# One load queue in the order of need, and x normalised between the steps of the context's projection

## The chip, the cores and the metric

The kernel runs on one core of a Trainium2 chip. The metric is the device time of one execution in microseconds, as the median of three runs. Engines are named as in the profile: PE is TensorE (PEld its weight load), DVE is VectorE, ACT is ScalarE, POOL is GpSimd, SP is SyncE; SPq and ACTq are the queues on which SP and ACT issue DMAs.

## The reference

Two transformer blocks on x (512 tokens by 1024), all in float32. The change touches only the beginning of the first one:

```
mod   = silu(c) @ w_ada + b_ada            # w_ada: 1024 x 6144, six vectors of 1024: shift, scale, ...
h     = rmsnorm(x,   g) * (1 + scale) + shift        # 512 x 1024, with c
h_ctx = rmsnorm(ctx, g) * (1 + scale) + shift        # 256 x 1024, with c_ctx
p     = h @ w_in,  p_ctx = h_ctx @ w_in              # w_in: 1024 x 10304
# columns of p: q, k, v, z, then xBC (a convolution of 5 taps over tokens, then silu), dt, gates
# then neighbourhood attention, a state-space scan seeded by the context's states, 16 experts;
# then a second block of two layers
```

The context is needed first: its B and its x columns of xBC give the states with which the scan of x begins.

## The kernel before, in words

Matrix products keep float32 precision by splitting both operands into a high and a low part; one "step" of the projection is three matmuls (high by high, low by high, high by low; `mm3`, L331 to L333) of one k-tile. `Stream` holds an ordered list of units (a set of weight columns with its steps). Raw weights (`raw`, 2 buffers) come by DMA on SPq; ACT makes the high part (`wh`, L200), DVE or, every second time once `pool_share` is 2, POOL the low part (`wl`, L220), a pair of k-tiles at a time, five pairs at most. `st.count` counts steps; `st.defer(n, f)` runs `f` n steps later, and all that `f` issues then stands in the in-order queues of its engines behind what was issued before. `st.wait = 14` keeps a pair from being split until its raw load was issued 14 steps ago, and `st.stop` with `pump_some` splits pairs by hand.

The order of units at the beginning: `ub` (B columns for the context, 32 steps of 256 tokens), `udt` (dt columns: 8 steps for the context, 8 for x), `us[0]` to `us[3]` (x columns of xBC for the context, 32 steps each), then `qk_unit(0)`, the first that needs x in earnest. After each half of a 32-step unit comes `conv` (L760 on ACT twice, then L765 on DVE eight times), and after the second half a Silu on ACT (L784).

Before the first step: `ident`, `va`, `vb`, the two tiles of ctx and the four of x are loaded on ACTq; the first 2048 columns of `w_ada` come on SPq as 16 tiles of 512 KB (`ada_load`, L667 to L671), in four groups along k. All six tiles are squared and normalised together (L701 to L705), transposed on PE (L716) to `cT` and `xT`, and `ada_mm` (L695) makes shift and scale, which L932 to L940 turn into columns. `modulate` (L730) then takes a tile k at a time: DVE scales and shifts (L732), ACT writes the high part (L737), DVE or POOL the low part (L738). For the context `pump_some` splits three further pairs of weights in between; for x, `modulate(0, ...)` calls `st.fill(1.0)` after each k, so that some three steps of `ub` run between two k.

The other 4096 columns of `w_ada` come in 16 tiles of 1 MB (`ada_load2`, L899) on ACTq; `ada_mm2(i)` (L905) multiplies tile i in between the steps: the first at step 20 (`ADA0`), one every 10 steps (`ADA`), tile i+3 being asked for 8 steps (`AL`) after tile i was used.

## Time and profile before

| what | us |
|---|---|
| median of 3 runs | 3430.79 (3430.62 to 3438.5) |
| the profiled execution, its own time | 3432.32 |
| its span in the trace | 3430.5 |
| PE busy in the span | 3208.5 (94%) |
| DVE, ACT, POOL busy | 1624.5, 1168.1, 554.2 |

Times inside the trace are counted from the start of the span; the execution's own time is 1.8 us longer than the span. The change lies in the first 5% of it. A PE that is busy need not be at its full clock: the granted clock (PEclk) is 1.00 at 2.4 GHz and 0.50 at 1.2 GHz.

### The profile page before, as it was taken

Reading aid. Unit: us, or ns where it says so; the run is one execution under the profiler, and the core shown is the slowest. Engines: PE = TensorE matmul, PEld = TensorE weight load, DVE = VectorE, ACT = ScalarE, POOL = GpSimd, SP = SyncE. Lnnn points to the kernel's source line nnn. Section 1 sums busy time; section 2 is a strip of 40 time slices with the busy share of each in tenths; the row PEclk is TensorE's granted clock in tenths of the full one; section 3 lists DMA queues with packets and bytes.
Section 4 is the critical chain, followed back from the end, with each engine's and each line's share of the span. In section 5 each row is a group of like instructions: output and inputs, shape, how many; then the busy total and the mean of one; then the engine's idle time right before and its main releaser. Section 6 shows DMA issues by size and latency. Waiting matters only on the chain. (4 is left out here: it accounts for less than half of the span.)

```text
span 3430.5 us, 42023 instructions
## 1 busy us (share of the span) xinstructions
PE 3208.5 (94%) x16365; PEld 2207.9 (64%) x16365; DVE 1624.5 (47%) x3113; ACT 1168.1 (34%) x2064; POOL 554.2 (16%) x371
## 2 busy tenths in 40 slices
PE   7999999999899898888889888999999999999998
PEld 4778877777678543324324224777888877788887
DVE  5745557676554410111011015776544467765444
ACT  4455545555323100100000003555433355543332
POOL 2232213444110100000000000241111103401111
PEclk9999999999999899999999999999999999999999
DMA  8622122222444799999999996212323221123232
GB/s 293 237 65 79 59 79 79 83 80 77 146 147 184 310 410 418 420 421 421 421 421 421 421 421 227 68 47 71 93 92 105 92 88 56 41 84 99 92 92 80
DMA packets 223389, 646.64 MB, mean 188 GB/s; under 512 B 17973, under 2 KB 110253, under 8 KB 171349
## 3 DMA queue, kind: packets, MB, share of 16 engines
q1 hardware_dynamic: 211176, 607.26, 46.6%
q10 hardware_dynamic: 12013, 36.69, 3.0%
q8 instruction: 129, 2.11, 0.3%
q14 instruction: 71, 0.58, 0.0%
HBM read 628.67 MB, written 15.21 MB: 188 GB/s over the span
## 5 line engine op out<-in xcount | busy, mean ns | idle before, releaser
L1968 PE MATMUL hd<-xw,xe 128*64 128x512 f32 x2048 | 462.8, 595 | 63.1 <-DMA xw<-in_w_up_dram 42.1
L220 DVE TENSOR_TENSOR wl<-raw,wh 128x1024 fp32r<-128x1024 f32 (+1 forms) x306 | 377.9, 1249 | 124.3 <-ACT wh L200 122.8
L200 ACT ACTIVATE wh<-raw 128x1024 fp32r<-128x1024 f32 (+1 forms) x349 | 343.4, 1003 | 212.2 <-PE psg L333 133.1
L331 PE MATMUL psg<-HA,wh 128*128 128x512 f32 (+1 forms) x1024 | 392.6, 383 | 0.0
L332 PE MATMUL psg<-HB,wh 128*128 128x512 f32 (+1 forms) x1024 | 387.7, 379 | 3.9 <-DVE HB L467 3.9
L333 PE MATMUL psg<-HA,wl 128*128 128x512 f32 (+1 forms) x1024 | 388.0, 379 | 0.0
L1968 PEld LDWEIGHTS hd<-xw,xe 128*64 128x64 f32 x2048 | 151.6, 137 | 363.4 <-issue 241.2
L2009 PE MATMUL down<-xw,hidT 128*64 128x512 f32 x1024 | 237.8, 600 | 36.5 <-DMA xw<-in_w_down_dram 36.4
L331 PE MATMUL psg<-h_hi,wh 128*128 128x512 f32 x584 | 255.3, 437 | 1.1 <-DVE vsb L1334 0.9
L333 PE MATMUL psg<-h_hi,wl 128*128 128x512 f32 x584 | 236.9, 406 | 0.0
L332 PE MATMUL psg<-h_lo,wh 128*128 128x512 f32 x584 | 236.5, 405 | 0.0
L332 PEld LDWEIGHTS psg<-HB,wh 128*128 128x128 f32 x1024 | 195.0, 190 | 38.6 <-DVE HB L467 4.7
L333 PEld LDWEIGHTS psg<-HA,wl 128*128 128x128 f32 x1024 | 194.6, 190 | 35.9
L331 PEld LDWEIGHTS psg<-HA,wh 128*128 128x128 f32 x1024 | 195.7, 191 | 33.8
L2009 PEld LDWEIGHTS down<-xw,hidT 128*64 128x64 f32 x1024 | 75.0, 137 | 188.1 <-issue 120.6
L2627 POOL TENSOR_TENSOR va<-va,ga 128x512 f32<-128x512 f32 x44 | 90.9, 2066 | 546.1 <-DVE va L2609 546.0
L2024 ACT ACTIVATE yh<-down,gcol 128x512 fp32r<-128x512 f32 x16 | 11.0, 686 | 489.4 <-PE down L2009 489.4
L1980 DVE TENSOR_TENSOR hid<-hid,hd 128x512 f32<-128x512 f32 x32 | 22.0, 687 | 314.0 <-PE hd L1968 313.9
L2043 POOL TENSOR_TENSOR Y<-Y,R 128x512 f32<-128x512 f32 x4 | 5.0, 1275 | 966.4 <-ACT tmp L2041 966.4
L220 POOL TENSOR_TENSOR wl<-raw,wh 128x1024 fp32r<-128x1024 f32 (+1 forms) x43 | 101.7, 2368 | 291.2 <-ACT wh L200 291.2
L331 PE MATMUL psg<-wh,hidh 128*128 128x512 f32 x352 | 139.5, 396 | 0.0
L333 PE MATMUL psg<-wh,hidl 128*128 128x512 f32 x352 | 139.2, 396 | 0.0
(487 smaller groups left out, 5979.3 us busy)
## 6 DMA issues: line engine op xcount, KB each, us to landing
xw<-in_w_gate_dram SPq DMA_DIRECT2D x128, 1024.0 KB, 19.8
xw<-in_w_up_dram SPq DMA_DIRECT2D x128, 1024.0 KB, 19.8
xw<-in_w_down_dram SPq DMA_DIRECT2D x126, 1024.0 KB, 19.8
raw<-in_w_up_dram SPq DMA_DIRECT2D x176, 256.0 KB, 3.7
raw<-in_w_in_dram SPq DMA_DIRECT2D x34, 1024.0 KB, 5.2
raw<-in_w_in_dram SPq DMA_DIRECT2D x96, 256.0 KB, 3.1
raw<-in_w_down_dram SPq DMA_DIRECT2D x44, 512.0 KB, 4.3
raw<-in_w_in_dram SPq DMA_DIRECT2D x33, 512.0 KB, 4.7
```

The source lines that it names most:

```text
L200: nc.scalar.activation(wh[:, :kn, :nco], src, AF.Copy)
L220: eng.tensor_tensor(wl[:, :kn, :nco], src, wh[:, :kn, :nco].bitcast(F32), op=ALU.subtract)
L331: nc.tensor.matmul(ps, l, r, start=first, stop=False, skip_group_check=skip)
L332: nc.tensor.matmul(ps, l, rh, start=False, stop=False, skip_group_check=skip)
L333: nc.tensor.matmul(ps, lh, r, start=False, stop=last, skip_group_check=skip)
L1968: P.matmul(ps[c][64 * e:64 * e + 64], xe[p // 2][k // 2 % 2][:, 2 * (k // 4) + k % 2, c0:c0 + 64], self.tiles[p, w, k, e][:, 512 * c:512 * ...
L1980: V.tensor_tensor(acts[p, c], acts[p, c], ps[c], op=ALU.mult)
L2009: P.matmul(down[h][64 * e:64 * e + 64], b[:, 64 * e:64 * e + 64], w[:, 1024 * r + 512 * h:1024 * r + 512 * h + 512], start=j == 0 and r == ...
L2024: S.activation(hi, down[h], AF.Copy, scale=gates[p])
L2043: G.tensor_tensor(o, o, R3[:, :512], op=ALU.mult)
L2627: G.tensor_tensor(v, v, g[j], op=ALU.mult)
```

## The change

All first loads go on SPq, in this order: `ident`, `va`, `vb`, ctx, then `w_ada` as 1 MB tiles of 128 rows by 2048 columns (six buffers; tiles 6 and 7 are issued after the matmuls of tiles 0 and 1), the two raw tiles of `ub`, and only then x. Before the first step only the context is squared, normalised and transposed. `kb.warm` adds five matmuls of `ident` by itself behind the last `ada` matmul and 14 behind the four transposes of L932. The vectors of shift and scale are made before the first pair of weights is split, and the low parts of the context alternate between DVE and POOL.

x is worked on inside the projection: squares at steps 14 to 20, its `rsqrt` at 26, the four row scalings (`by_r`) at 28 to 34, and `x_turn(k)` at steps 42, 45, ... 63. `x_turn` transposes one k into a PSUM bank of tag `m` (there are two), DVE scales and shifts from PSUM, ACT makes the high part, DVE or POOL the low one. The dt columns for x become a unit of their own, `udtx`, after `us[0]`, which loads and splits these weight columns a second time. The first `ada_mm2` moves from step 20 to step 48, the spacing from 10 steps to 8, and the first three `ada_load2` from before the first step to steps 26, 32 and 38.

```diff
--- before.py
+++ after.py
@@ -572,8 +572,8 @@
 LAG = 4
 RT = (12, 15)
 WAIT = 14
-ADA = 10
-ADA0 = 20
+ADA = 8
+ADA0 = 48
 CS = (20, 22, 50, 54)
 FN = 4.6
 ORD = "tsn"
@@ -589,8 +589,8 @@
 NT = ('o', 's', 'm', 's')
 ROT = "gsmgsms"
 AQ = 20
-AL = 8
-SX = 56
+AL = 4
+SX = 28
 VT_ = 't'
 VD = 16
 NG = 3
@@ -617,7 +617,7 @@
 
     keep = es.enter_context(tc.tile_pool(name="keep", bufs=1))
     ident = keep.tile([128, 128], F32, name="ident")
-    S.dma_start(ident, A["ident"])
+    nc.sync.dma_start(ident, A["ident"])
     kb.ident = ident
     wx = ExitStack()
     wp = wx.enter_context(tc.tile_pool(name="wp", bufs=1, reuse_waits="tile"))
@@ -656,26 +656,23 @@
     p0 = zero.enter_context(tc.tile_pool(name="p0", bufs=1, side="right"))
     va = p0.tile([128, 128], F32, name="va")
     vb = p0.tile([120, 128], F32, name="vb")
-    S.dma_start(va, A["vec_a"])
-    S.dma_start(vb, A["vec_b"])
-    xT = p0.tile([128, 8, T], F32, name="xT")
+    nc.sync.dma_start(va, A["vec_a"])
+    nc.sync.dma_start(vb, A["vec_b"])
+    xx = p0.tile([128, 4, D], F32, name="xx")
     cT = p0.tile([128, 8, TC], F32, name="cT")
     raw = ExitStack()
     p00 = raw.enter_context(tc.tile_pool(name="p00", bufs=1, side="right"))
-    aw = {}
-
-    def ada_load(kh):
-        for j in range(4):
-            t = p00.tile([128, 2, 512], F32, tag="aw", bufs=8, name="aw")
-            nc.sync.dma_start(t, A["w_ada"][256 * kh:256 * kh + 256, 512 * j:512 * j + 512].rearrange("(k p) f -> p k f", p=128))
-            aw[kh, j] = t
-
-    ada_load(0)
-    ada_load(1)
-    xt = p00.tile([128, 6, D], F32, name="xt")
-    for t in (4, 5, 0, 1, 2, 3):
-        src = A["x"][128 * t:128 * t + 128] if t < 4 else A["ctx"][128 * (t - 4):128 * (t - 4) + 128]
-        S.dma_start(xt[:, t], src)
+    xt = p00.tile([128, 2, D], F32, name="xt")
+    for t in range(2):
+        nc.sync.dma_start(xt[:, t], A["ctx"][128 * t:128 * t + 128])
+    aw = []
+
+    def ada_load(k):
+        aw.append(p00.tile([128, 4, 512], F32, tag="aw", bufs=6, name="aw"))
+        nc.sync.dma_start(aw[k], A["w_ada"][128 * k:128 * k + 128, :2048].rearrange("p (j f) -> p j f", f=512))
+
+    for k in range(6):
+        ada_load(k)
     tri = p1.tile([128, 3, 128], F32, name="tri")
     sel = p1.tile([128, 24], F32, name="sel")
     dtv, acs, dte, Eac, cdec = (p1.tile([128, 6, 64], F32, name=n_) for n_ in "dtv acs dte Eac cdec".split())
@@ -689,41 +686,51 @@
     S.activation(sil[:, :, 0:2].rearrange("p k v -> p v k"), cols[:, 112:128].rearrange("p (v k) -> p v k", v=2), AF.Silu)
     ada_ps = PS.bank([128, 512], F32, "o", "ada")
 
-    def ada_mm(kh):
-        for k in range(2):
-            for j in range(4):
-                P.matmul(ada_ps[32 * j:32 * j + 32], sil[:, 2 * kh + k], aw[kh, j][:, k],
-                         start=kh == 0 and k == 0, stop=kh == 3 and k == 1, skip_group_check=True)
-
     ss = p0.tile([128, 6], F32, name="ss")
-    junk = xT[:, 0:2].rearrange("p a b -> p (a b)")
-    for t in (4, 5, 0, 1, 2, 3):
-        S.activation(junk, xt[:, t], AF.Square, accum_out=ss[:, t:t + 1])
-    V.tensor_scalar(ss, ss, 1.0 / D, EPS, op0=ALU.mult, op1=ALU.add)
-    rs = kb.rsqrt(ss, 6, p0)
-    for t in (4, 5, 0, 1, 2, 3):
-        V.tensor_scalar(xt[:, t], xt[:, t], rs[:, t:t + 1], None, op0=ALU.mult)
-    ada_mm(0)
-    ada_load(2)
-    ada_mm(1)
-    ada_load(3)
+    junk = cT[:, 0:4].rearrange("p a b -> p (a b)")
+    for t in range(2):
+        S.activation(junk, xt[:, t], AF.Square, accum_out=ss[:, 4 + t:5 + t])
     S.dma_start(tri, A["tri"])
     S.dma_start(sel, A["sel"])
-    for n in range(12):
+
+    def row_r(t0, n):
+
+        v = ss[:, t0:t0 + n]
+        V.tensor_scalar(v, v, 1.0 / D, EPS, op0=ALU.mult, op1=ALU.add)
+        return kb.rsqrt(v, n, p0)
+
+    def by_r(x, r):
+        V.tensor_scalar(x, x, r, None, op0=ALU.mult)
+
+    rc = row_r(4, 2)
+    for t in range(2):
+        by_r(xt[:, t], rc[:, t:t + 1])
+    for n in range(4):
         ps = PS.bank([128, 512], F32, "gsm"[n % 3], "xTp")
         for i in range(4):
-            k, t = (2 * n + i // 2, 4 + i % 2) if n < 4 else (n - 4, i)
-            P.transpose(ps[:, 128 * i:128 * i + 128], xt[:, t, 128 * k:128 * k + 128], ident)
-        if n < 4:
-            o, v = cT[:, 2 * n:2 * n + 2].rearrange("p a b -> p (a b)"), ps
+            P.transpose(ps[:, 128 * i:128 * i + 128], xt[:, i % 2, 256 * n + 128 * (i // 2):256 * n + 128 * (i // 2) + 128], ident)
+        o = cT[:, 2 * n:2 * n + 2].rearrange("p a b -> p (a b)")
+        if n % 2:
+            V.tensor_copy(o, ps)
         else:
-            o, v = in_time(xT[:, n - 4]), ps.rearrange("p (r g c) -> p r g c", g=8, r=8)
-        if n % 2:
-            V.tensor_copy(o, v)
-        else:
-            S.activation(o, v, AF.Copy)
-    ada_mm(2)
-    ada_mm(3)
+            S.activation(o, ps, AF.Copy)
+    for k in range(8):
+        for j in range(4):
+            P.matmul(ada_ps[32 * j:32 * j + 32], sil[:, k], aw[k][:, j], start=k == 0, stop=k == 7, skip_group_check=True)
+        if k < 2:
+            ada_load(6 + k)
+    kb.warm("m", 5)
+
+    def x_turn(k):
+
+        ps = PS.bank([128, 512], F32, "m", "xTp")
+        for t in range(4):
+            P.transpose(ps[:, 128 * t:128 * t + 128], xx[:, t, 128 * k:128 * k + 128], ident)
+        o = cT[:, 2 * (k % 4):2 * (k % 4) + 2].rearrange("p a b -> p (a b)")
+        V.tensor_scalar(in_time(o), ps.rearrange("p (r g c) -> p r g c", g=8, r=8), gsc[:, 0, k:k + 1], shc[:, 0, k:k + 1],
+                        op0=ALU.mult, op1=ALU.add)
+        S.activation(h_hi[:, k], o, AF.Copy)
+        (G if k % 2 else V).tensor_tensor(h_lo[:, k], o, h_hi[:, k].bitcast(F32), op=ALU.subtract)
     mod0 = p0.tile([128, 512], F32, name="mod0")
     V.tensor_copy(mod0, ada_ps)
     raw.close()
@@ -735,7 +742,7 @@
             if k < 7:
                 scale(k + 1)
             S.activation(hi[:, k], src[:, k], AF.Copy)
-            (G if k % 2 or v else V).tensor_tensor(lo[:, k], src[:, k], hi[:, k].bitcast(F32), op=ALU.subtract)
+            (G if k % 2 else V).tensor_tensor(lo[:, k], src[:, k], hi[:, k].bitcast(F32), op=ALU.subtract)
             each(k)
 
 
@@ -830,12 +837,12 @@
         ops += [lambda: stt(d, d, 1.0, s, op0=ALU.add, op1=ALU.mult),
                 lambda: stt(dtv[:, tk].rearrange("p t h -> p (t h)"), d, 2.0, xr, op0=ALU.mult, op1=ALU.add),
                 lambda: stt(th(na), dtv[:, tk], -1.0, alog[:, None, :].to_broadcast([128, nt, 64]), op0=ALU.mult, op1=ALU.mult),
-               ] + [None] * (16 if t0 else 38) + [
+               ] + [None] * (16 if t0 else 30) + [
                 sums, None, None,
                 lambda: S.activation(dte[:, tk], dte[:, tk], AF.Exp)]
         return ops
 
-    udt = Unit([([(0, A["w_in"][:, ODT:ODT + 128])], 8)], 128)
+    udt, udtx = (Unit([([(0, A["w_in"][:, ODT:ODT + 128])], 8)], 128) for _ in range(2))
 
     def spread(n0, ops, every=1):
         for i, f in enumerate(ops):
@@ -845,7 +852,7 @@
     def ev_dtc(ps):
         V.tensor_copy(dtT[:, T:], ps[:64, :TC])
         tt = lambda *a: V.tensor_tensor(*a, op=ALU.mult)
-        spread(14, dt_ops(4, 2) + [lambda: tt(ddc, dtv[:, 4:6], dte[:, 4:6]),
+        spread(6, dt_ops(4, 2) + [lambda: tt(ddc, dtv[:, 4:6], dte[:, 4:6]),
                                   lambda: tt(ddc[:, 0, :32], ddc[:, 0, :32], cdec[:, 5, :32]),
                                   lambda: tt(ddc[:, 1, 32:], ddc[:, 1, 32:], cdec[:, 4, 32:])])
     kb.group_b(udt, 0, act_c, TC, ev_dtc)
@@ -853,8 +860,9 @@
     def ev_dtx(ps):
         V.tensor_copy(dtT[:, :T], ps[:64, :T])
         spread(SX, dt_ops(0, 4))
-    kb.group_b(udt, 0, act_t, T, ev_dtx)
-    udt.steps = [(0, 2 * p + r, c, f) for p, r, c, f in udt.steps]
+    kb.group_b(udtx, 0, act_t, T, ev_dtx)
+    for u in (udt, udtx):
+        u.steps = [(0, 2 * p + r, c, f) for p, r, c, f in u.steps]
 
     def b_nat():
         def part(t):
@@ -924,12 +932,15 @@
 
     st.stop = True
     ub = xbc_unit(OB, 16, bcT, b_nat)
+    for t in range(4):
+        nc.sync.dma_start(xx[:, t], A["x"][128 * t:128 * t + 128])
     st.add(udt)
     us = [xc_unit(0)]
-    st.pump_some(1)
+    st.add(udtx)
     ptm = PS.bank([128, 512], F32, "t", "ptm")
     for m in range(4):
         P.transpose(ptm[:, 128 * m:128 * m + 128], mod0[:, 128 * m:128 * m + 128], ident)
+    kb.warm("m", 14)
     shc = p0.tile([128, 2, 8], F32, name="shc")
     gsc = p0.tile([128, 2, 8], F32, name="gsc")
     for v in (1, 0):
@@ -938,8 +949,7 @@
         V.tensor_tensor(shc[:, v].rearrange("p (j m) -> p j m", m=4), pv[:, 0:2], b4[:, 0], op=ALU.add)
         V.tensor_tensor(gsc[:, v].rearrange("p (j m) -> p j m", m=4), pv[:, 2:4], b4[:, 1], op=ALU.add)
         V.scalar_tensor_tensor(gsc[:, v], gsc[:, v], 1.0, cols[:, 0:8], op0=ALU.add, op1=ALU.mult)
-    for i in range(3):
-        ada_load2(i)
+    st.pump_some(1)
     modulate(1, cT, c_hi, c_lo, lambda k: k in (1, 3, 5) and st.pump_some(1))
     st.stop = False
     st.wait = WAIT
@@ -948,11 +958,20 @@
     kb.rot = ["g", "s"]
     st.defer(ADA0, lambda: ada_mm2(0))
     S.activation(alog, alog, AF.Exp)
-    modulate(0, xT, h_hi, h_lo, lambda k: st.fill(1.0))
-    zero.close()
+    for i in range(3):
+        st.defer(26 + 6 * i, lambda i=i: ada_load2(i))
+    rx_ = []
+    for t in range(4):
+        st.defer(14 + 2 * t, lambda t=t: S.activation(junk, xx[:, t], AF.Square, accum_out=ss[:, t:t + 1]))
+        st.defer(28 + 2 * t, lambda t=t: by_r(xx[:, t], rx_[0][:, t:t + 1]))
+    st.defer(26, lambda: rx_.append(row_r(0, 4)))
+    for k in range(8):
+        st.defer(42 + 3 * k, lambda k=k: x_turn(k))
     for g in range(1, 4):
         us.append(xc_unit(g))
         st.finish(us[g - 1])
+        if g == 1:
+            zero.close()
 
     shuf = [(i + 16) % 32 for i in range(32)]
     units, made, QK, VU, VT = {}, [0], {}, {}, {}
```

## Rows read from the trace of the kernel before

**Rows 1.** Busy time by stretch (us; count), TensorE clock, DMA share, GB/s.
```profile
18.00:36.00 18.00, 14.74 (x93) 7.21 (x93) 9.88 (x24) 5.70 (x10) 0.00 (x0) 0.91 1.05 385
41.00:47.00 6.00, 4.75 (x20) 4.46 (x21) 3.73 (x8) 3.65 (x7) 3.69 (x4) 0.50 1.01 426
47.00:54.00 7.00, 4.15 (x28) 3.35 (x27) 4.87 (x7) 3.54 (x7) 4.60 (x4) 0.99 0.49 141
54.00:57.40 3.40, 3.40 (x21) 3.18 (x23) 2.58 (x3) 1.67 (x4) 1.28 (x1) 0.51 0.52 201
60.00:100.00 40.00, 39.11 (x292) 30.55 (x292) 35.08 (x63) 18.52 (x25) 15.90 (x7) 1.00 0.79 284
100.00:140.00 40.00, 36.74 (x262) 27.58 (x261) 34.62 (x65) 19.32 (x28) 9.56 (x4) 0.96 0.80 280
```

**Rows 2.** DMA issues of the first 40 us: KB each, median us to landing.
```profile
aw<-in_w_ada_dram SPq DMA_DIRECT2D x16, 512.0 KB, 7.6
xt<-in_x_dram ACTq DMA_DIRECT2D x4, 512.0 KB, 8.1
```

**Rows 3.** Timeline, from the last w_ada tile to the context's last high part.
```profile
35.37 1.90 PE L695 MATMUL ada<-aw,sil 128*32 128x512 f32 x10 [1.56 <-DMA aw<-in_w_ada_dram]
38.12 1.06 ACT L200 ACTIVATE wh<-raw 128x1024 fp32r<-128x1024 f32 x1 [7.41 <-DMA raw<-in_w_in_dram]
39.21 1.22 DVE L220 TENSOR_TENSOR wl<-raw,wh 128x1024 fp32r<-128x1024 f32 x1 [1.21 <-ACT wh L200]
41.55 0.73 ACT L737 ACTIVATE c_hi<-cT 128x256 fp32r<-128x256 f32 x2 [2.37 <-DVE cT L732]
42.02 0.58 PE L331 MATMUL psc<-c_hi,wh 128*128 128x256 f32 x1 [3.31 <-ACT c_hi L737]
...
52.10 0.42 ACT L737 ACTIVATE c_hi<-cT 128x256 fp32r<-128x256 f32 x1 [1.72 <-DVE cT L732]
52.54 1.28 ACT L950 ACT_TABLE_LOAD   x1
```

**Rows 4.** Groups by line and shape, 0 to 160 us: busy us, mean ns.
```profile
L220 DVE TENSOR_TENSOR wl<-raw,wh 128x1024 fp32r<-128x1024 f32 x14 | 21.1, 1510 | 11.5 <-ACT wh L200 11.5
L765 DVE SCALAR_TENSOR_TENSOR xc<-psc,cw,xc 128x254 f32<-128x254 f32 x30 | 14.4, 482 | 1.1
L701 ACT ACTIVATE xT<-xt 128x1024 f32<-128x1024 f32 x6 | 6.3, 1054 | 0.6 <-DMA xt<-in_x_dram 0.4
L732 DVE TENSOR_SCALAR xT<-xT,gsc,shc 128x512 f32<-128x512 f32 x8 | 9.1, 1163 | 0.0
L705 DVE TENSOR_SCALAR xt<-xt,rs_y 128x1024 f32<-128x1024 f32 x6 | 4.1, 750 | 0.0
L722 DVE COPY xT<-xTp 128x512 f32<-128x512 f32 x4 | 2.7, 688 | 0.4 <-PE xTp L716 0.4
L563 DVE SCALAR_TENSOR_TENSOR rs_t<-rs_y 128x6 f32<-128x6 f32 x3 | 0.5, 166 | 0.1
L760 ACT ACTIVATE bcT<-psc,cols,cw 128x256 f32<-128x256 f32 x4 | 2.0, 548 | 0.0
```

**Rows 5.** Timeline of PE: transposes, two steps, step 80, the end of `us[3]`.
```profile
24.74 5.77 PE L716 MATMUL xTp<-ident,xt 128*128 128x128 f32 x48
...
63.82 0.28 PE L331 MATMUL psg<-c_hi,wh 128*128 128x256 f32 x1
64.17 0.28 PE L331 MATMUL psg<-c_hi,wh 128*128 128x256 f32 x1
...
90.45 1.06 PE L911 MATMUL ada<-aw,sil 128*32 128x512 f32 x8
...
154.32 0.28 PE L331 MATMUL psg<-c_hi,wh 128*128 128x256 f32 x1
```

**Rows 6.** Timeline of ACT: two issues of w_ada's later tiles.
```profile
103.15 0.33 ACTq L903 DMA_DIRECT2D aw<-in_w_ada_dram  x1
...
114.09 0.33 ACTq L903 DMA_DIRECT2D aw<-in_w_ada_dram  x1
```

## The prediction

> **What bounds the kernel now.** I read the stretches first. Until about 36 us the DMA engines are full (share 1.05, 385 GB/s) while PE, DVE and ACT have gaps: the beginning is bound by bytes [rows 1]. Then the timeline: PE gets the last `w_ada` tile at 35.37, starts the first step at 42.02, and ACT starts the context's last high part only at 52.10 [rows 3]. In 47 to 54 PE is busy 4.15 of 7 us: it follows the context's `modulate`, not its own speed; then it runs 3.4 us at half clock, and from 60 to 100 it is busy 39.1 of 40 us [rows 1]. The reader should see the column beside it: DVE is busy 35.1 of the same 40 us, and 34.6 of the next 40. There PE paces the kernel, but DVE follows with almost no slack. That decides this change, because it moves work onto DVE and hangs PE on it. All later stages only start earlier or later by what is won or lost here.
>
> **The loads.** Ahead of the last `w_ada` tile came 8 MB of `w_ada` and 3 MB of ctx and x; x (four tiles of 512 KB, 2.1 MB [rows 2]) now comes behind it. At 385 GB/s that is 5.4 us [rows 1]. The tiles are now 1 MB with 8 KB per partition; the stretch with such tiles in flight ran at 426 GB/s [rows 1], which on 8.4 MB would save 2.1 us more. Ends 5.4 and 7.5, taken 7.2, near the upper one: the tiles of that stretch have the shape of the new ones.
>
> **From the last tile to the end of the first half of `ub`.** Four matmuls remain after the last tile instead of ten, and the shift and scale are ready before the first pair of weights. But that pair still waits for its raw tile, which landed 2.75 us after the last `w_ada` tile, and then for wh 1.06, wl 1.22, one scaling, one high part (about 1 us): 6 us instead of 6.65 [rows 3]. Gain 0.7. In the half itself each two k cost wh, wl, a scaling and a high part in turn, 1.06 + 1.22 + 0.8 = 3.1 us, whoever makes the low part; 10.5 us pass between the first and the last high part [rows 3]. I give 0.5 for the low parts on DVE. The half ended near 54.0; it should end at 54.0 - 7.2 - 0.7 - 0.5 = 45.6, 8.4 us earlier. The 19 warm matmuls stand where PE waits for DVE and for the raw tile; if the five delay L932, by at most five transposes' worth, 0.6 us [rows 5].
>
> **x between the steps.** This is the step that costs. Between the end of the context's last high part (1.5 us before the half ends) and `x_turn(0)`, in order on ACT before the first convolution: a table load 1.28 (the Exp of `alog`), wh 1.06, a square 1.05, the convolution's first part 0.55: 3.9 us [rows 3, 4]. Then on DVE: eight taps of 0.48, 3.9; wl 1.2; `rsqrt` with its scaling, 12 small operations of 0.17, 2.0; wl 1.2; two row scalings of 0.75, 1.5; the second half's eight taps, issued at step 31, 3.9; two more row scalings, issued at 32 and 34, 1.5. Together 15.2 us [rows 3, 4]. So `x_turn(0)` can start at 45.6 - 1.5 + 3.9 + 15.2 = 63.2. PE needs for the 26 steps up to it 26 x 0.35 = 9.1 us [rows 5], and is there at 54.7. **It waits 8.5 us**, with all later steps queued behind four transposes.
>
> Then PE may do `x_turn(0)`, three steps and `x_turn(1)`, 2.05 us. Next come the transposes of dt at step 45, which need one of the two `m` banks, that is, the first scaling of x from PSUM. On DVE that stands behind wl of the second dt load, whose wh on ACT stands behind the Silu of B: table load 1.28, Silu 1.05, two wh 2.1, two issues 0.7, wl 1.2, the scaling 0.69, from 61.7 [rows 3, 4, 6]: 68.7. PE has been ready since 65.3: **3.4 us more.** By the clock rows a PE that has stood still 3.3 us resumes at 0.50 [rows 1, 3]; at that clock the 2.05 us are 4.1 and still fit. The Trainium skill, "TensorE: Matmul & The Clock Gate", section "HAM oscillation — how this bites in real kernels", says the same of idle gaps; by it the stall would be paid once more in slow matmuls, by these rows that payment lies inside the second wait.
>
> From step 45 to 80: 27 steps 9.5, six `x_turn` of four transposes 2.9, ten other transposes 1.2, four `ada_mm2` 4.2, eight steps of 512 tokens at 0.70, 5.6: 23.4 us [rows 5]. `x_turn(7)` needs the bank of `x_turn(5)`, whose scaling stands behind eight more taps (3.9) from step 55. Ends 0 and 5 (taps and what had queued), taken 3. Step 80 comes at 68.7 + 23.4 + 3 = 95.1, with four tiles of `ada_mm2` done; before it came at 90.45 with six [rows 5]. On equal footing (two of 1.06) that is 97.2: **6.8 us behind**, although the half ended 8.4 ahead. Of this, 3.9 us are the 32 transposes of x themselves (0.12 each [rows 5]), which lay under the loads before.
>
> The scaling of x is not dearer on DVE: a pass of 128x512 out of PSUM took 0.69, eight are 5.5, where the SBUF form here took 9.1 for eight [rows 4]. The Trainium skill, "VectorE: DVE Perf Modes", section "Why PSUM operands drop a tier", says that a float32 operand in PSUM loses the two-port mode, so the move would cost; with the SBUF form at half of 0.69 it would be 2.7 us more on DVE and about as much behind. The trace does not bear that out for this stretch, where POOL works beside it.
>
> **After step 80.** The work is the same. PE lost there before: 3.3 us idle in 100 to 140, and 1.6 us by a mean clock of 0.96 [rows 1]. These losses come where DVE has a backlog; after the stall PE no longer runs ahead of DVE, so I take 4.5 of the 4.9 as won back (ends 0 and 4.9). `ada_mm2` ends at step 168 instead of 170, nothing. Sum: +6.8 - 4.5 = +2.3 us on the profiled 3432.3, so 3434.6; the median of the runs stands 1.5 below that execution, so **3433**.
>
> **Rivals.**
> - *PE is not held* (14%). The row scalings are done when PE arrives at step 42. Then step 80 gains 8.4, loses 3.9 for the transposes, and gets back 3.8: from 54.0 to 90.45 PE's own work was 32.6 (24 steps 8.4, eight long ones 5.6, 32 steps 11.2, six `ada_mm2` 6.4, transposes 1.0 [rows 5]). With 4.5 later: 12.8 less, 3418. For it: DVE was idle 2.1 of the 7 us up to 54 [rows 1]. Against it: 15.2 us of DVE work in 9.1 us of PE work, in one queue. It decides when `x_turn(0)` starts by 55.
> - *Half the waits* (12%): if ACT and DVE interlock less than I add up, 15 us of waits become 7 or 8, and the kernel gains 5: about 3426.
> - *The later tiles of `w_ada` come late* (12%), the other side. A tile now has 20 steps from its issue to its use, before 22. A step with all that goes with it took 63.9 / 96 = 0.67 us [rows 5], so 13.3 us instead of 14.6. Two issues 10 steps apart (6.7 us) ran 10.9 apart behind waits on ACT, 4.2 late [rows 6], and a landing under load takes 8.1 [rows 2]: 12.3. There is 1 us to spare. Beyond 13.3 each of the twelve last tiles stops PE; at 1 us each the kernel is at 3445. Against it: bytes alone, 1.57 MB per 8 steps of 5.3 us, are 296 GB/s, under 385.
> - *My forecast* (62%), with its own range 3424 to 3440: the load's ends (minus 0.3, plus 1.8), the third stall (minus 3, plus 2), what is won back (plus 4.5).
>
> **How the numbers follow.** 0.3% of this kernel is 10.3 us, about what a measurement of it tells from no change: faster means under 3420.5, slower over 3441. The first rival alone is faster, the third alone slower; the forecast and the half case lie within. Faster 0.14, same 0.74, slower 0.12. The range, 3420 to 3442, leaves out half of the first rival and most of the third.
>
> **What would show it.** Right: ctx squared before 10 us; the last first-stage `w_ada` tile near 28; the first step near 34; x's transposes waiting on DVE's row scaling for several us near step 42, with DVE full from the first convolution on; PE's waits in 100 to 140 mostly gone. Wrong: no wait before the first transposes of x; or the last tile after 30 (the queue does not order the bytes); or `ada_mm2` waiting for DMA.

## The result: slower by 20 us, in two losses of some 10 each

The changed kernel takes 3451.09 us (median of 4 runs, 3449.26 to 3454.55), the one before, beside it, 3430.70 (4 runs, 3428.17 to 3438.5): a ratio of 1.0059 (95% interval 1.0046 to 1.0071). The forecast was 3433 with a range up to 3442, so the result lies outside it. The profiled span grew from 3430.5 to 3447.5 us.

Where the time goes is read by asking both traces when the same line runs (in the changed kernel all lines behind L760 stand 7 to 19 lower down; the marks bear their numbers of before, the lines shown from a trace those of its own kernel). Five marks are enough: the load of the rotary table (L1048), the first copy L1334 in the scan, the first expert matmul L1968, the last one L2009, and the last L2627 in the second block. Figures after the first row are microseconds behind the kernel before.

| kernel | L1048 | L1334 | L1968 | L2009 | L2627 |
|---|---|---|---|---|---|
| before | 162.2 | 654.0 | 1167.6 | 2097.3 | 3369.4 |
| after | +10.0 | +11.3 | +20.2 | +20.2 | +17.0 |

The first loss, 10 us, is complete by 162. Then little happens until 654 (1.3 more). The second, 9 us, falls between 654 and 1168, in the scan, whose code and data the change does not touch. Each row of marks is one execution: the 3.2 that come back in the second block here do not come back in the run without row scalings (19.3, then 19.2), so no reading rests on them.

The beginning, by windows of the changed kernel (length; busy us and count on PE, PEld, DVE, ACT, POOL; mean PE clock; DMA share; GB/s), to be held against [rows 1]:

```profile
18.00:28.00 10.00, 6.60 (x40) 0.72 (x32) 0.00 (x0) 0.00 (x0) 0.00 (x0) 0.74 1.01 419
60.00:100.00 40.00, 27.80 (x168) 20.39 (x169) 28.26 (x51) 15.72 (x22) 9.97 (x7) 0.74 0.50 173
100.00:140.00 40.00, 40.00 (x287) 29.32 (x285) 30.63 (x59) 19.36 (x27) 10.71 (x4) 1.00 0.91 319
```

The loads run at 419 GB/s. From 60 to 100 PE is busy 27.8 us at a mean clock of 0.74, where it was busy 39.1 at full clock; from 100 to 140 it is full, where it had lost 3.3. The loss lies in the middle row. PE's timeline of the changed kernel, the rows behind a wait and four milestones (start, length, what, count; in brackets the idle time before, and what ended it):

```profile
28.61 1.58 PE L719 MATMUL ada<-aw,sil 128*32 128x512 f32 x8 [0.57 <-DMA aw<-in_w_ada_dram]
...
34.85 0.38 PE L331 MATMUL psc<-c_hi,wh 128*128 128x256 f32 x1
...
60.11 1.05 PE L728 MATMUL xTp<-ident,xx 128*128 128x128 f32 x2 [5.23 <-DVE xx L703]
65.23 0.48 PE L728 MATMUL xTp<-ident,xx 128*128 128x128 f32 x1 [4.08 <-DVE xx L703]
65.89 0.48 PE L728 MATMUL xTp<-ident,xx 128*128 128x128 f32 x1 [0.18 <-DVE xx L703]
...
72.18 0.47 PE L812 MATMUL dtn<-ident,dtT 64*128 64x64 f32 x2 [3.04 <-DVE cT L730]
...
90.13 0.66 PE L728 MATMUL xTp<-ident,xx 128*128 128x128 f32 x4 [3.75 <-DVE cT L730]
...
91.71 1.11 PE L871 MATMUL bct<-ident,bcT 128*128 128x128 f32 x4 [0.92 <-DVE cT L730]
...
98.94 0.49 PE L331 MATMUL psg<-h_hi,wh 128*128 128x512 f32 x1
...
164.58 0.28 PE L331 MATMUL psg<-c_hi,wh 128*128 128x256 f32 x1
```

The last `w_ada` tile is used at 28.61 (forecast 28.2), the first step starts at 34.85 (near 34). Then come the waits that were forecast, at the forecast places, but later: 9.5 us for 8.5, 3.0 for 3.4 and 4.7 for 3; the first step of `udtx` (step 72) comes at 98.94, where the forecast has 95.1 - 5.6 = 89.5. At 164.58 `us[3]` ends, 10.3 behind [rows 5].

What PE waits for stands on DVE, with POOL beside it (timelines of the changed kernel):

```profile
48.55 3.98 DVE L772 SCALAR_TENSOR_TENSOR bcT<-psc,cw,bcT 128x255 f32<-128x255 f32 x8 [4.62 <-ACT bcT L767]
52.45 1.22 DVE L220 TENSOR_TENSOR wl<-raw,wh 128x1024 fp32r<-128x1024 f32 x1
...
53.78 2.37 DVE L560 TENSOR_SCALAR rs_t<-ss 128x4 int32<-128x4 int32 x1
56.19 0.17 DVE L561 TENSOR_SCALAR rs_y<-rs_t 128x4 int32<-128x4 int32 x1
...
60.54 3.97 DVE L772 SCALAR_TENSOR_TENSOR bcT<-psc,cw,bcT 128x255 f32<-128x255 f32 x8
64.43 1.41 DVE L703 TENSOR_SCALAR xx<-xx,rs_y 128x1024 f32<-128x1024 f32 x2
65.75 0.41 DVE L853 COPY dtT<-psg 64x256 f32<-64x256 f32 x1
68.87 2.53 DVE L220 TENSOR_TENSOR wl<-raw,wh 128x1024 fp32r<-128x1024 f32 x1 [2.71 <-ACT wh L200]
71.32 0.80 DVE L730 TENSOR_SCALAR cT<-xTp,gsc,shc 128x512 f32<-128x512 f32 x1
```

```profile
53.76 2.36 POOL L220 TENSOR_TENSOR wl<-raw,wh 128x1024 fp32r<-128x1024 f32 x1 [4.71 <-ACT wh L200]
67.97 2.35 POOL L220 TENSOR_TENSOR wl<-raw,wh 128x1024 fp32r<-128x1024 f32 x1 [11.84 <-ACT wh L200]
```

Two rows are dearer than forecast. An operation on 128 x 4 elements, whose neighbour of the same size takes 0.17, takes 2.37 us and ends at 56.15, as POOL's `wl` ends at 56.12. And a `wl` of 1.22 takes 2.53 from 68.87 on, while POOL's second `wl` runs until 70.32. That reads as if DVE stood still each time until POOL was done; two runs below, without POOL's low parts, test it.

### The profile page after: what moved, and what is told of

It reads as the page before. It is cut to its first block, busy times and chain, and to the rows that moved or that the text cites. A ratio compares the mean times of both kernels' runs of the same rounds, so it can differ in the third digit from the quotient of the medians.

```text
span 3447.5 us, 42098 instructions
## 1 busy us (share of the span) xinstructions
PE 3213.0 (93%) x16403; PEld 2212.2 (64%) x16403; DVE 1622.1 (47%) x3127; ACT 1167.5 (34%) x2061; POOL 544.1 (16%) x366
## 5 line engine op out<-in xcount | busy, mean ns | idle before, releaser
L220 DVE TENSOR_TENSOR wl<-raw,wh 128x1024 fp32r<-128x1024 f32 (+1 forms) x308 | 387.0, 1271 | 123.4 <-ACT wh L200 122.3
L1999 DVE TENSOR_TENSOR hid<-hid,hd 128x512 f32<-128x512 f32 x32 | 21.8, 688 | 312.6 <-PE hd L1987 312.4
```

What stands on the lines that cost most here:

```text
L220: eng.tensor_tensor(wl[:, :kn, :nco], src, wh[:, :kn, :nco].bitcast(F32), op=ALU.subtract)
L1999: V.tensor_tensor(acts[p, c], acts[p, c], ps[c], op=ALU.mult)
```

## The experiments on the second loss: which pair POOL splits

The scan's waits differ between the traces in a way that names a suspect. The view of waits of the changed kernel, 500 to 1180 us (PE's wait, total us, times, longest):

```profile
PE psg L331 <- ACT wh L200: 6.6, 1, 6.6
...
PE psg L333 <- POOL wl L220: 2.5, 2, 1.9
...
PE stp L1409 <- POOL xd L1398: 2.1, 2, 1.5
...
PE psg L331 <- DVE xs L772: 1.6, 1, 1.6
```

In the kernel before, over 490 to 1170, the first is shorter, and the other three are not in the list:

```profile
PE psg L331 <- ACT wh L200: 4.1, 1, 4.1
```

`Stream` gives POOL every second low part by the parity of a running number: `pair_i % pool_share == 0`. `udtx` brings one more pair of weights, so from the tenth pair on the parity is turned round to the end of that stream: POOL now splits the first pair of each raw tile, which PE needs soonest, in 2.4 us instead of DVE's 1.2. Four kernels test this.

**Dealing turned back, and turned round without the change (first try).** In the changed kernel, and in the one before:

```diff
-  self.pair_i % self.pool_share == 0
+  (self.pair_i - (self.pair_i > 9)) % self.pool_share == 0     # changed kernel
+  (self.pair_i + (self.pair_i >= 9)) % self.pool_share == 0    # kernel before
```

> The changed kernel, in which the extra pair of weights of udtx is not counted when every second low part goes to POOL, so that all later pairs fall to the engine that made them in the kernel before. Theory of two losses (about 10 us between steps 42 and 72, about 8 us more between 650 and 960 us, the second from the flipped split between DVE and POOL): about 3443, the lag at 215 us still near 10, at 1130 us 10 to 12 instead of 19. Rival, that the second loss comes from the later start alone: 3451 as the changed kernel, lag at 1130 us still near 19.

> The kernel before, in which the split is flipped from the first pair of us[1] on, and nothing else. Theory of two losses: about 7 to 8 us slower than before, 3438, all of it after 650 us. Rival of the later start: no change, 3431.

Measured: 3451.85 (1.0061, 1.0047 to 1.0075) and 3450.93 (1.0056, 1.0043 to 1.0068). Neither is what the theory said, and the totals alone would have sunk it. The marks show why not:

| kernel | L1048 | L1334 | L1968 | L2009 | L2627 |
|---|---|---|---|---|---|
| after, dealing turned back everywhere | +11.2 | +13.3 | +13.9 | +14.0 | +22.8 |
| before, dealing turned round everywhere | +1.5 | +4.0 | +10.6 | +10.6 | +19.2 |

Between 654 and 1168 the one no longer loses 9 us and the other now loses 7, as the theory says. But both lose some 9 us in the second block: it has a `Stream` of its own, whose numbering the change had never moved, and the edit turned that round too. So the edit was wrong, not the theory, and it was made again for the first stream alone (`raw_bufs == 2` marks it):

```diff
+  (self.pair_i - (self.raw_bufs == 2 and self.pair_i > 9)) % self.pool_share == 0     # changed kernel
+  (self.pair_i + (self.raw_bufs == 2 and self.pair_i >= 9)) % self.pool_share == 0    # kernel before
```

> The changed kernel, with the low parts of the first stream's weight pairs dealt to POOL and VectorE as in the kernel before: pairs from the tenth on count as if the second dt unit had brought none. The second block has a stream of its own, which the change never touched and which is left as it is here (in the run that took the flip out everywhere it was turned round). Theory of two losses: the first 10 us stay, lost by step 80 and still behind at 162 us; the loss of 8 to 9 us between 650 and 960 us is gone, and the second block runs as before, so the end is 10 to 13 us behind the kernel before: 3441 to 3443. Rival, that the time goes back to some pattern of the clock whatever the order: no change, 3451.

> The kernel before, with only the dealing of the low parts turned round from the tenth weight pair of the first stream on; nothing else of the change, and the second block untouched. Parity theory: 8 to 10 us slower than the kernel before, most of it lost between 650 and 1170 us: 3439 to 3441. Rival, that the loss needs the changed beginning: 3431, no change.

Measured: 3442.08 (1.0036, 1.0023 to 1.0048) and 3441.59 (1.0031, 1.0019 to 1.0043), the first inside its expectation, the second 0.6 above it.

| kernel | L1048 | L1334 | L1968 | L2009 | L2627 |
|---|---|---|---|---|---|
| after, first stream turned back | +10.5 | +12.0 | +10.0 | +9.8 | +9.9 |
| before, first stream turned round | +0.2 | +2.1 | +11.3 | +11.5 | +11.6 |

The waits go with the dealing, not with the change: the kernel before with the first stream turned round shows the same four lines in 490 to 1170 us, with 6.6, 2.5, 1.9 and 1.6, and the changed kernel with it turned back has 3.8 for the first, 0.3 for the last, and neither of the others. They exceed those of before by 8.5. Where the time goes is better read in windows, since some other waits are shorter. The kernel before, turned round:

```profile
500.00:560.00 60.00, 56.35 (x232) 41.35 (x231) 44.57 (x64) 30.57 (x47) 24.61 (x17) 1.00 0.21 71
800.00:860.00 60.00, 56.78 (x248) 39.76 (x247) 34.92 (x58) 27.92 (x51) 28.98 (x23) 0.97 0.17 62
920.00:980.00 60.00, 53.34 (x216) 41.43 (x215) 36.51 (x52) 20.28 (x28) 4.99 (x2) 0.91 0.69 240
```

The kernel before:

```profile
500.00:560.00 60.00, 57.99 (x240) 42.61 (x239) 45.17 (x64) 30.74 (x47) 22.45 (x17) 1.00 0.21 71
800.00:860.00 60.00, 59.43 (x286) 41.88 (x285) 36.24 (x50) 33.29 (x56) 33.33 (x23) 1.00 0.18 66
920.00:980.00 60.00, 54.67 (x227) 42.37 (x226) 41.71 (x57) 18.72 (x26) 5.68 (x2) 0.97 0.60 211
```

By eight windows of 60 us from 500 to 980 PE's idle time grows from 16.2 to 22.2, and the lower clock takes 0.03 x 56.8 + 0.06 x 53.3 = 4.9 more: 10.9 together, where the marks give 11.1 from 162 to 1168. The second loss is shown: 9 to 11 us for the parity of a counter. By what path the dealing lengthens the longest of the waits is not shown: it is one for a high part, at 979 us in the changed kernel, where POOL splits none of the pairs beside it.

## The experiments on the first loss: PE's waits between steps 42 and 72

Each of the following takes one link away from what holds PE. The numbers that decide stand in one table behind them. Those marked * have the first stream's dealing turned back and are to be held against 3442, the others against 3451.

**Row scalings left out** (x stays unnormalised):

```diff
-        st.defer(28 + 2 * t, lambda t=t: by_r(xx[:, t], rx_[0][:, t:t + 1]))
```

> The changed kernel without the four row scalings of x (x goes on unnormalised). If the whole chain over ACT and DVE holds PE (taps, splits, Silu, second dt split, then the first scaling out of PSUM), the wait before the first transposes of x goes, but the wait at the dt transposes takes its place and ends only 1.5 us earlier: 2 to 4 us gained, 3447 to 3449. Rival, that the row scalings are what costs: the 9.5 us of waits on them are gained, about 3441.

Measured: 3449.91 (1.0055, 1.0042 to 1.0069), 1.2 below the changed kernel, which is less than that kernel's own runs differ, and 0.9 above the chain's 3447 to 3449. x's transposes no longer wait, and the dt transposes three steps on wait 13.6 instead of 3.0, until the same time:

```profile
71.69 0.47 PE L812 MATMUL dtn<-ident,dtT 64*128 64x64 f32 x2 [13.63 <-DVE cT L730]
```

**Silu of B ten steps later**, so that ACT makes the high parts behind it sooner:

```diff
-  S.activation(out, out, AF.Silu); after()
+  def end(): S.activation(out, out, AF.Silu); after()
+  st.defer(10, end) if ch0 == 16 else end()
```

> The changed kernel; the Silu of B's first half, with its table load, is put off by ten steps, so that the weight high parts behind it on ScalarE are not held by the convolution. Theory that the chain ScalarE to VectorE holds the dt transposes at step 45: they start near 68 instead of 72.2 us, and 3 to 4 us are won, 3447. Rival, that VectorE alone with all its taps is what PE waits for: the dt transposes start within 1 us of where they did, 3451.

Measured: 3448.59 (1.0052, 1.0038 to 1.0065), 2.5 below the changed kernel, with intervals that overlap, and 1.6 above the chain's 3447. It did not come by the way that the chain named: the dt transposes started at 71.40, without a wait, since PE came there late. With wh free, POOL's `wl` moved under the row scalings, and two of them took 3.49 us instead of 1.41:

```profile
59.46 3.49 DVE L703 TENSOR_SCALAR xx<-xx,rs_y 128x1024 f32<-128x1024 f32 x2
```

**x's rows before the convolution** *: squares in ACT's gaps of the context, `rsqrt` and row scalings right behind, the Exp of `alog` later, and Silu ten steps later.

> The changed kernel, low parts dealt as before in the first stream, Silu of B ten steps later, and x's row work ahead of the convolution: two squares in ScalarE's gaps of the context's last pairs, two behind them, rsqrt and the four row scalings on VectorE right after, where it was idle 4.6 us waiting for the convolution's first part; the Exp of alog with its table load goes behind. By the theory that the order on ScalarE and VectorE is what holds PE at steps 42 and 45: x's first transposes start without a wait near 55 us, the dt transposes near 64 instead of 72, and the kernel ends 6 to 9 us below 3442, at 3433 to 3436. Rival, that the amount of VectorE work up to 100 us is the bound and its order is not: PE waits as long, two places further on, and the end is 3440 to 3442.

Measured: 3443.21 (1.0040, 1.0026 to 1.0053): far from the forecast, 1.2 above the rival's 3442. x's transposes went without a wait, and PE waited 6.5 us for a low part that now stood behind x's rows, then 5.1 for the dt transposes and 4.2 at a later `x_turn`. The rows took longer than counted, since two small operations of the `rsqrt` stood still, each beside one of POOL's low parts (from 47.30 to 49.70 and from 50.40 to 52.79):

```profile
60.85 0.58 PE L333 MATMUL psc<-c_hi,wl 128*128 128x256 f32 x1 [6.45 <-DVE wl L220]
```

```profile
47.31 2.42 DVE L565 SCALAR_TENSOR_TENSOR rs_y<-rs_t,rs_y 128x4 f32<-128x4 f32 x1
...
50.54 2.27 DVE L564 TENSOR_TENSOR rs_t<-rs_t,ss 128x4 f32<-128x4 f32 x1
```

**No low part on POOL in this stretch** *: the first ten pairs all split on DVE, in the changed kernel's order and with x's rows before the convolution.

> The changed kernel, low parts dealt as before in the first stream (3442 without more), but the first ten pairs all split on VectorE, so that GpSimd has none until the second dt unit. By the theory that GpSimd's subtraction stops VectorE: no operation of the rsqrt above 0.2 us, every low part 1.22; 3.5 us of standing still go and three low parts of 1.2 come, so the dt transposes start within 1 us of 72.6 and the end is 3441 to 3443. Rival, that the long operations have another cause: rsqrt's 2.37 stays, the three low parts come on top, dt transposes near 76, 3444 to 3446.

> The kernel with x's rows ahead of the convolution (3443.2), and the first ten pairs all split on VectorE. There GpSimd's low parts stopped the rsqrt twice, 2.42 and 2.27 us, and a low part took some 3 us for 1.2 later: by the theory 6 us of standing still go and 3.6 us of low parts come. x's rows end near 53 instead of 55.7, PE's wait for a low part is 3 to 5 instead of 6.5, and the end is 3440 to 3442. Rival: rsqrt stays at 6.5 us in all, and the end is 3444 or more.

Measured: 3442.80 (1.0037, 1.0024 to 1.0049) and 3441.76 (1.0030, 1.0019 to 1.0041), as the theory gave. Every operation of the `rsqrt` is back at 0.16 to 0.17 us, every low part at 1.21 to 1.23, each pair of row scalings at some 1.4. In the changed kernel's order:

```profile
55.79 0.17 DVE L560 TENSOR_SCALAR rs_t<-ss 128x4 int32<-128x4 int32 x1
...
67.72 1.23 DVE L220 TENSOR_TENSOR wl<-raw,wh 128x1024 fp32r<-128x1024 f32 x1 [3.41 <-ACT wh L200]
```

So POOL does stop DVE; but the three low parts come on top of DVE's work, and nothing is won. With x's rows ahead PE now waits 9.0 us for the dt transposes.

**x further back** *: `x_turn(k)` at 62 + 5k, `udtx` behind `us[1]` (its later work 4 steps behind it, `SX`, instead of 28), and Silu later.

> The changed kernel with x's transposes and its dt unit behind the next unit of x_c: x_turn(k) at step 62 + 5k instead of 42 + 3k, the second dt unit one unit later, Silu of B ten steps later, and the dealing of low parts as in the kernel before. By the theory that the first loss is the wait of PE for VectorE between steps 42 and 45, and the second the dealing, both go: the first product stays 7 us earlier, 3.9 us of it go to x's transposes, and the kernel ends at 3425 to 3432, at or below the kernel before. Rival, that VectorE's work in the first 100 us is the bound wherever x stands: the loss of some 10 us comes only later, 3440 to 3443.

Measured: 3456.96 (1.0075, 1.0063 to 1.0088), worse than any other and outside both expectations. The transposes of the context's dt had stayed at step 45, and waited 11.8 us there for the copy of `dtT` (L853 in the changed kernel), which stands on DVE behind the taps of B's second half and x's last two row scalings; two `x_turn` waited 8.4 more.

**Row scalings out and Silu later** *, the two links together (x unnormalised).

> The changed kernel, low parts dealt as before in the first stream, with the row scalings of x left out (x stays unnormalised) and the Silu of B ten steps later: the two links together that were taken out singly. Theory of a chain with two parallel arms, each of which holds PE when the other is gone: the dt transposes start near 66 instead of 72 us and the end is 3434 to 3437. Rival, that a third arm of nearly the same length stands behind them (the taps of the second half): the gain is that of the later Silu alone, 2 to 3 us, 3439 to 3440.

Measured: 3436.10 (1.0019, 1.0010 to 1.0028), as the theory of two arms gave: 6 us won, more than the 1.2 and 2.5 of the two singly. The dt transposes come at 67.97, two later than it gave, and PE waits 10.7 us before them.

**x's transposes off PE** * (the scaling reads x's rows untransposed, which is not the reference's computation):

```diff
-  ps = PS.bank(...); for t in range(4): P.transpose(ps[...], xx[:, t, ...], ident)
+  ps = xx[:, k % 4, 512 * (k // 4):512 * (k // 4) + 512]
```

> The changed kernel, low parts dealt as before in the first stream (3442 without more), with x's 32 transposes left out: the scaling reads x's rows untransposed, so its values are not those of the reference; all work of VectorE, ScalarE and POOL stays. Theory that PE is held because the transposes stand in its queue: no wait at step 42, the lag at 162 us goes from 10 behind to some 5 ahead, 3424 to 3428. Rival, that VectorE's and ScalarE's own work bounds this stretch: only the 3.9 us of the transposes and part of the bank's wait go, the lag stays 4 to 7 behind, 3435 to 3438.

Measured: 3438.22 (1.0020, 1.0011 to 1.0029), 0.2 above the rival's upper end. Even without x's transposes in its queue PE is held at step 45:

```profile
66.35 0.47 PE L810 MATMUL dtn<-ident,dtT 64*128 64x64 f32 x2 [9.65 <-DVE dtT L851]
```

**Products of the identity in PE's waits** *, to keep its clock up: 36, 28 and 20, then 20, 16 and 18 of them.

> The changed kernel, low parts dealt as before in the first stream (3442 without more), with products of the identity added on TensorE inside the waits that the change made: 36 ahead of x's first transposes, 28 between its second and third, 20 ahead of the second four. They are written to a part of the bank that the transposes overwrite. By the reading that 4.5 us of the first loss are matmuls at the lower clock after the waits: the clock is 1.0 from 66 us on, the first step of the second dt unit comes 3 to 5 us earlier, 3438. Rival, that VectorE paces this stretch and PE at full clock only waits longer at the next place: within 1 us of 3442.

> As the run with products of the identity inside PE's waits, but 20, 16 and 18 of them instead of 36, 28 and 20: a product took 0.24 us there, and the waits are 5.2, 4.1 and some 4 us. By the reading that matmuls at half clock after the waits are 4.5 us of the first loss: x's first transposes where they were, the clock 1.0 from 60 us on, and 2 to 4 us won: 3438 to 3440. Rival, that PE at full clock only waits longer at the next place: within 1 us of 3442.

Measured: 3446.80 (1.0050, 1.0037 to 1.0062) and 3442.85 (1.0034, 1.0021 to 1.0047). The first put in 19 us of products, more than the waits, and delayed PE itself. The second fits the waits, though the dt transposes came 0.6 later than without them; the time is the rival's, within 1 us of 3442. Its windows show full clock up to 80 us, and a lower one behind:

```profile
60.00:80.00 20.00, 17.64 (x148) 15.47 (x147) 14.80 (x26) 7.62 (x9) 3.64 (x2) 1.00 0.59 214
80.00:100.00 20.00, 13.11 (x81) 9.79 (x81) 12.81 (x29) 7.78 (x12) 5.73 (x4) 0.74 0.31 106
```

Without the products (dealing turned back alone):

```profile
60.00:80.00 20.00, 12.03 (x60) 8.78 (x61) 12.92 (x21) 7.72 (x9) 3.62 (x2) 0.57 0.58 210
80.00:100.00 20.00, 12.83 (x91) 9.53 (x90) 14.13 (x32) 7.40 (x12) 4.38 (x4) 0.83 0.31 106
```

All together (times of the trace; waits of PE from 40 to 120 us by the view of waits, the context's included; behind the kernel before at L1048):

| kernel | x's first transposes | dt transposes | `udtx` | PE's waits | L1048 |
|---|---|---|---|---|---|
| before | - | 76.59 | - | 10.2 | 162.2 |
| after | 60.11, 65.23 | 72.18 | 98.94 | 19.4 | +10.0 |
| * dealing turned back | 60.55, 65.67 | 72.61 | 101.96 | 21.8 | +10.5 |
| rows out | 55.70 | 71.69 | 99.48 | 20.4 | +10.6 |
| Silu later | 62.44, 67.56 | 71.40 | 96.14 | 17.8 | +7.4 |
| * rows before the convolution | 61.87 | 70.22 | 95.69 | 18.0 | +10.7 |
| * rows out, Silu later | 55.02 | 67.97 | 94.91 | 16.5 | +5.1 |
| * transposes off PE | none | 66.35 | 84.99 | 19.9 | +6.2 |
| * 20, 16, 18 products | 61.01, 66.22 | 73.18 | 101.57 | 11.4 | +10.1 |
| * POOL's low parts on DVE | 59.9 | 73.25 | 100.65 | 22.5 | +9.5 |

Whatever is taken away, PE's waits stay at 16 to 23 us, where they were 10 before; they move. (With the products they fall to 11, because PE is busy with work that counts for nothing.) PE comes to step 42 near 55 us, and what it asks for there hangs on DVE from four sides: row scalings, the low parts behind Silu, the bank that the first scaling frees, and the copy of `dtT`. The last has nothing to do with x: its transposes were also brought forward, from 14 steps behind the dt columns to 6. No run put that move back by itself.

## The experiments on the loads

**Second-stage tiles of `w_ada` as early as before**: `ADA` 10, `ADA0` 20, `AL` 8, first loads at steps 2, 4 and 6.

> The changed kernel with the times of w_ada's later tiles as before: first loads at steps 2, 4 and 6, first product at step 20, then every 10 steps, loads 8 steps after. Theory of the held PE: three products then lie in front of the wait at step 42, where PE has time, and two fewer behind it: 2 to 3 us gained, 3448. My third rival (late tiles) finds no wait of PE on such a tile in the changed kernel's trace and so predicts no change here; more than 5 us gained would speak for some cost of the spacing that the waits do not show.

Measured: 3451.31 (1.0060, 1.0046 to 1.0074), no gain. The first product waited 3.4 us for its tile, and the dt transposes came at 76.32.

**The tiles' form alone, in the kernel before**: eight tiles of 128 rows in four buffers.

```diff
-  t = p00.tile([128, 2, 512], F32, tag="aw", bufs=8, name="aw")       # 16 loads
+  aw[k] = p00.tile([128, 4, 512], F32, tag="aw", bufs=4, name="aw")   # 8 loads
```

> The kernel before with one part of the change alone: the first stage's w_ada in eight tiles of 128 rows (1 MB, 8 KB for each partition) in four buffers instead of sixteen column tiles of 512 KB in eight; queues, x, steps and dealing as before. By the reading that the tiles' form gave 2 of the 7 us: the last tile is used 1 to 2 us before 35.4, and the end is 3429. Rival, that all of the gain was x's bytes moved behind: no change of that time within 0.5 us, 3430.5.

Measured: 3436.93 (1.0020, 1.0011 to 1.0028), slower by 7, which neither reading had. x still came on ACT's queue, beside the new tiles on SP's, and now came late: ACT's squares of x follow each other as the tiles land.

```profile
16.27 1.06 ACT L697 ACTIVATE xT<-xt 128x1024 f32<-128x1024 f32 x1 [1.04 <-DMA xt<-in_x_dram]
...
20.04 1.06 ACT L697 ACTIVATE xT<-xt 128x1024 f32<-128x1024 f32 x1 [2.62 <-DMA xt<-in_x_dram]
...
23.80 1.06 ACT L697 ACTIVATE xT<-xt 128x1024 f32<-128x1024 f32 x1 [2.61 <-DMA xt<-in_x_dram]
...
27.56 1.06 ACT L697 ACTIVATE xT<-xt 128x1024 f32<-128x1024 f32 x1 [2.61 <-DMA xt<-in_x_dram]
```

One tile of 512 KB in 3.76 us is 139 GB/s, a third of the 421 that all queues moved from 16 to 28 us. In the kernel before the last square starts at 19.41. The rows of the tiles on SP's queue had gone from 2 KB to 8, x's on the other stayed at 4. The Trainium skill, "DMA: Bandwidth & Descriptors", section "Queues, rings and completion order", says that a DMA engine takes turns between queues packet by packet. If the packets of the two queues are as 4 to 8, as their rows are, x would get a third, an estimate that agrees; no run here varied the size by itself.

**Order and form of the loads alone, in the kernel before**: one queue, ctx and x ahead of the tiles, x's rows and transposes ahead of the stream as before.

```diff
-        S.dma_start(xt[:, t], src)          # after the first tiles, on ACT's queue
+        nc.sync.dma_start(xt[:, t], src)    # ahead of them
```

> The kernel before with the order and form of the loads alone: everything on one queue, ctx and x ahead of w_ada, w_ada in eight tiles of 128 rows; x's rows and transposes ahead of the stream as before, steps and dealing as before. In the run with the tiles' form alone, x came one tile in 3.8 us on its own queue beside them and the transposes ended at 40. If the order on one queue is what the tiles' form needs: x's squares end before 14 us, the last w_ada product near 33, the first step near 40 instead of 42, and the kernel is 1 to 3 us below the one before, 3428 to 3429. Rival, that bytes alone count: no change, 3430.

Measured: 3429.18 (11 runs, 3425.06 to 3432.92) beside 3430.54: a ratio of 0.9993 (0.9985 to 1.0002). The last square of x starts at 13.34 and the last `w_ada` products end at 35.6, but the first step starts at 41.61, 0.4 earlier and not 2, behind a wait of 4.5 that goes back to the first raw tile. It is the best kernel of the study, by 1.4 us that its interval does not tell from nothing.

## Why the prediction was wrong, point by point

- **The loads, and up to the half's end: right.** 28.61 for 28.2 and 34.85 for 34; the first convolution starts on ACT at 47.52, near the 47.4 of the sum (45.6 - 1.5 + 3.9 - 0.55).
- **The first wait: right place, too short.** The sum gave 63.2 for the last row scaling's end; the transposes that hang on the last two start at 65.23 and 65.89. The 12 small operations were priced at 0.17 each; one took 2.37 beside POOL's `wl`, which accounts for 2.2 of it.
- **The second wait: right place, 3.5 us late.** 72.18 for 68.7: 2 us carried over, and 1.3 because `wl` took 2.53 beside POOL. In the trace of before the same hold was to be seen only as scalings that took more than twice their time [rows 4].
- **From 45 to 80: the term of 3 us and the clock.** The later waits were 4.7 us. Over 72.18 to 98.94 PE was busy 22.1 us at a mean clock of 0.84, 3.5 us of it slowness. "By these rows that payment lies inside the second wait" held for the first wait: the slow matmuls from 66.02 end at 69.1. It was not all: the second and the third wait were followed by slow matmuls of their own (72.18 to 77.4 at a clock of 0.50, 90.13 to 94.9 at 0.64), which the sum had at nothing. With 3.5 carried over and 1.7 of longer waits that is 8.7 of the 9.4 by which `udtx` came late. What the clock costs by itself is not shown: with the first waits filled it was full up to 80 us and lower behind, and `udtx` came only 0.4 earlier.
- **Step 80.** It came at 105.71, where the sum has 95.1; with the two `ada_mm2` still owed that is 17.4 behind, not 6.8. Of the 10.6 more, 9.4 stood before `udtx`, and 1.2 came in its eight steps (6.8 us for 5.6).
- **What is won back: right, and more.** From 100 to 165 PE was busy all 65 us, before 59.7; by the end of `us[3]` it came back from 17.4 behind to 10.3, 7.1 where the forecast had 4.5.
- **"After step 80. The work is the same": this step failed, and with it the range.** The work is the same, its dealing is not. The second copy of the dt weights was counted as split twice, but not as one more number in the counter that decides who splits. This costs 9 of the 20 us: 3451.09 with it, 3442.08 with the first stream dealt as before. The other part that failed is the sum up to step 80: its mechanism, PE held by DVE, is what the trace shows, but its size was 10.6 us too small, of which the larger gain behind it gave 2.6 back.
- **The dear scaling out of PSUM.** "The scaling of x is not dearer on DVE" holds against [rows 4], but the transposes' run puts a price on it: 0.54 us from SBUF against 0.81 from PSUM, medians of eight. The Trainium skill, "VectorE: DVE Perf Modes", section "Why PSUM operands drop a tier", had the direction right; it is some 2 us in eight. The 0.69 of the forecast was that of a plain copy.
- **The rivals.** PE was held for 9.5 us at step 42, so neither "PE is not held" nor "Half the waits" came true. That `w_ada`'s later tiles come late did not happen: no wait on them in 40 to 140. The forecast's own ends were added wrongly: 0.3 and 3 below and 1.8, 2 and 4.5 above 3433 give 3430 to 3441, not 3424 to 3440. The range's upper bound, 3442, is what the first loss comes to by itself; that it fits is luck, since the sum for that loss gave 3433.

What stays open is whether any order of x's work beats loading x first. The runs show that several links hold PE at nearly the same time; how the 10 us of the first loss divide between them is open, and no version without all of them was made.

## What to carry to other kernels

A queue that PE shares with others is only as early as the latest thing asked of them: before work is moved in between, add up, for each instruction that PE will meet, what stands ahead of its producer, and expect the second latest to take over when the latest is cured. Anything numbered (a parity, a round robin, a rotation) is part of the schedule: one more element shifts all that follows, 500 us away, and a twin stream that has its own counter must be left alone when this is tested. Compare runs by marks along the trace, since totals hid two effects of opposite sign.

## What the runs showed of the hardware that was not expected

DVE stands still until POOL's subtraction ends where the two meet in certain operations. A 128 x 4 operation took 2.24 to 2.42 us in twelve kernels instead of 0.17 and ended with POOL's; a subtraction took 2.53 instead of 1.22, two row scalings 3.49 instead of 1.41; without POOL's low parts there (two kernels) all were short. Eight taps, which read one operand from PSUM, took 3.98 in the kernel before from 59.91 on, with a low part on POOL from 59.34 to 61.94: they were not stopped. The Trainium skill, "SBUF — State Buffer", section "Who interferes with whom", gives the rule: the two engines share a pair of ports as an exclusive lock, which a DVE operation needs if it has two operands in SBUF or runs in a two-port mode. The rows agree, down to an operation of four columns.
